# The second layer's modulation summed by VectorE and Pool instead of TensorE

## The chip, the core and the metric

The kernel runs on one core of a Trainium2 chip. The metric is the device time of one execution in microseconds. Engines are named as in the profile: PE is TensorE's matmul (PEld its weight load), DVE is VectorE, ACT is ScalarE, POOL is Pool, SP issues DMAs from its own queue.

## What is computed

One step of a trunk of two layers on 640 tokens (128 context tokens, 512 latents) with 1024 features. Each layer has a mixer and a convolutional FFN, and each of the two is wrapped in norms whose shift, scale and gate come from a conditioning vector. There are two conditions, one for the context and one for the latents. The part that the change touches is this one, for layer 1:

```
def modulation(cond, w_mod, b_mod):
    m = (jax.nn.silu(cond) @ w_mod + b_mod)[:, None, :]
    return jnp.split(m, N_MOD, axis=-1)
...
sh1p, sc1p, gt1p, sh2p, sc2p, gt2p = modulation(ctx_cond, w_mod, b_mod)
sh1s, sc1s, gt1s, sh2s, sc2s, gt2s = modulation(c, w_mod, b_mod)
```

w_mod is 1024 x 6144 in float32, 25 MB, read once; only two rows are multiplied with it. Six groups of 1024 columns give the six vectors.

## The kernel before

The activations lie feature-major, 128 features on the partitions, as pairs of a rounded high and a low part; a product takes three matmuls (low x high, high x high, high x low). `split` makes such a pair of a loaded weight: ScalarE rounds (L310), VectorE subtracts (L311). Weights come in units of 512 KB through a ring of three raw buffers, issued by SP (L320).

The FFN (`ffn`) goes over 22 pairs of 128 columns. `up` makes both halves of a pair: `conv` loads and splits a unit of w_up, `feat` (L678) multiplies it in 48 matmuls into a pair of PSUM banks, then ScalarE (L1212) and VectorE (L1213, L1214) evacuate the banks with the three taps of the convolution. There are two pairs of banks in turn, so the product after next needs the evacuation of this one. ScalarE and VectorE then join the two halves (L1222, L1223) and split the result. After three or four pairs `down` multiplies them with w_down (mm3, L327 to L329) in ten steps of 512 columns into two banks in turn, and VectorE adds each step to the sum (L1244).

Layer 1's modulation runs in the background of layer 0's FFN: `ffn` takes a step of the generator `bg` between the two products of a pair (three pairs take one more). A step of `mod_steps` loads two pieces of w_mod of 128 x 1024 (L383, a ring of two buffers "mraw") and multiplies them at once: the two conditions, padded to 32 columns, are the weights, and four matmuls with 512 columns stand side by side in four column groups of the array (L386). Eight steps sum a group of 2048 columns over the input features in PSUM, and three groups make the six vectors; at the end of a group ScalarE copies the bank (L391), four transposes turn it and VectorE adds bias and gains. The gates go to DRAM as rows by a Pool DMA (L457).

The instructions of each engine stand in the order that a scheduler gave them when the kernel was built; on the chip each engine and each DMA queue keeps that order and waits where data or a buffer is missing.

Of the kernel before, what the change touches and what calls it, by code (L numbers as in the profile page):

```python
# [19 lines left out]
ALU = mybir.AluOpType  # L20
# [65 lines left out]
def turns(*gens):  # L86
    """the generators' steps in turn."""
    gens = list(gens)
    while gens:
        for g in list(gens):  # L90
            try:
                next(g)
            except StopIteration:
                gens.remove(g)
                continue
            yield


def weave(main, side, n=1):
    """after each step of main, n steps of side; what is left of side at the end."""  # L100
# [6 lines left out]
def play(order, **gens):  # L107
    """a step of the generator that each letter names; what is left of them at the end."""
# [5 lines left out]
def skew(gens, every=1, n=0):  # L114
    """generator i starts every steps behind generator i - 1; the first has gone n steps."""
# [9 lines left out]
class Arena:  # L125
    """Places buffers in the stretches of SBUF it has been given: large ones as high as they fit, others in the room
    given back longest ago.  A new user of some room waits only for the earlier users of the same room."""
# [35 lines left out]
    def fit(self, cols, x):  # L163
        """the bottom of the smallest free room in stretch x that has cols."""
# [18 lines left out]
class Chunks:  # L183
    """chunks of 128 features on the partitions, kept as pieces."""
# [10 lines left out]
class Cols:  # L195
    """the same, as one piece per stretch of columns (piece j: columns starts[j] ..)."""
# [7 lines left out]
    def parts(self, c0, c1):  # L204
        """(a, b, piece, column in it): columns a .. b of c0 .. c1 as they lie in the pieces."""
# [6 lines left out]
class Kernel:  # L212
# [6 lines left out]
    def open(self, name, n, cols, dt=F32, order=None, top=False, at=None):  # L219
        """a ring of n slots (at: the stretch of each; as a tuple: at its end)."""  # L220
# [21 lines left out]
    def trim(self, name, keep):  # L242
        """gives back all slots but the keep last ones got."""
# [26 lines left out]
    def zone(self, name, side, arena, sizes, dt):  # L270
        """a stretch of SBUF for one arena; close_zone ends it."""
# [60 lines left out]
    def rstd(self, ss, n, scale):  # L332
        """(scale * ss + eps) ** -0.5 by three Newton steps."""
# [17 lines left out]
    def rstd1(self, ss, scale):  # L351
        """(scale * ss + eps) ** -0.5 of one column: ScalarE's root, VectorE's reciprocal and a Newton step."""
# [9 lines left out]
    def exp_ln(self, after):  # L362
        """ScalarE's table with both Exp and Ln, loaded behind an instruction of its."""
# [10 lines left out]
    def mod_steps(self, l, g):  # L374
        """2048 columns of silu(c) @ w_mod, four column groups side by side in the PE array; then what follows from them."""
# [32 lines left out]

    def mod_first(self, h, A, B, behind):
        """layer 0's first shift and scale for quarter h of the features."""  # L410
# [35 lines left out]
    def gate_rows(self, l, qb, cols, bcol, gcol):  # L446
        """(gate + b) * g_post of both conditions, written to DRAM as rows."""
# [11 lines left out]
    def gates(self, l, qb):  # L459
        """those rows, the same in all partitions: [P, 1024] per condition."""  # L460
# [6 lines left out]
    def transpose_mod(self, xt, xn, i, A, B, hi, lo, off, bank="un", act=False, dve=2):  # L467
        """rmsnorm, modulation and transposition of one token tile into hi / lo columns off.. (xn: scratch)."""
# [41 lines left out]
    def residual(self, xt, t, m, G, junk=None):  # L510
        """xt += G * rmsnorm(m)."""
# [39 lines left out]
    def operand(self, name, order=None):  # L551
        """a product's feature-major operand, as two parts (high, low) of two pieces each."""
# [4 lines left out]
    def operand_cols(self, name, starts, w):  # L557
        """the same, as one piece per stretch of w columns."""
# [4 lines left out]
    def start(self):  # L563
        """conditioning vectors, first modulation group, normalised and transposed inputs, layer 0's first operand."""
# [58 lines left out]
    def first_vectors(self, l, r):  # L623
        """the columns that the first modulation needs."""
# [5 lines left out]
    def other_vectors(self, l, r):  # L630
        """the other vectors of a layer: a step to load them as rows, one to turn them."""
# [565 lines left out]
    def ffn(self, l, h2, G, bg, pre, store, fin, post):  # L1197
# [57 lines left out]
        for gi, n in enumerate(gsz):  # L1255
            want = NF if gi == len(gsz) - 2 else min(NF, f0 + n + 1)
            while nx < want:
                up(nx)
                nx += 1
                if nx in (10, 14, 18):  # L1260
                    next(bg, None)
# [457 lines left out]
```

## Time and profile before

| | us |
|---|---|
| median of 3 runs | 1807.58 (1804.44 to 1813.03) |
| span of the profiled execution | 1802.6 |
| TensorE busy | 1759.0 (98%) |
| VectorE busy | 1033.5 (57%) |
| ScalarE busy | 727.8 (40%) |
| Pool busy | 73.8 (4%) |

The page gives the profiled execution's span, from its first to its last instruction; its median run is 5 us longer. Busy shares are means over stages with different limits; the stage that matters is layer 0's FFN, whose up and down products run from about 495 to 990 us.

### The profile page before, as it was taken

The page shows a single profiled execution, that of the slowest core. Times are in us where ns is not written, and L with a number is a line of the kernel's source. Part 1 is how long each engine was busy: PE and PEld are TensorE (multiplying, and loading weights), DVE is VectorE, ACT ScalarE, POOL GpSimd, SP SyncE. Part 2 cuts the span into 40 slices and gives each one's busy share as a digit, 9 for nine tenths or more (in the row PEclk, how much of TensorE's full clock was granted, in tenths as well). Part 3 has the DMA queues.
Part 4 walks back from the last instruction along what each step waited for, and adds up shares of the span by engine and source line. Part 5 has one row for each costly group of instructions (what it writes and reads, how often), then busy time and mean ns, then how long its engine had stood idle before and what let it go on. Part 6 is the DMA issues. An engine that isn't in the chain of part 4 may idle for free.

```text
span 1802.6 us, 26680 instructions
## 1 busy us (share of the span) xinstructions
PE 1759.0 (98%) x10810; PEld 1525.6 (85%) x10810; DVE 1033.5 (57%) x1950; ACT 727.8 (40%) x1291; POOL 73.8 (4%) x177
## 2 busy tenths in 40 slices
PE   6999999989999999999999999999999999999998
PEld 4787888757798989898988988887889989898996
DVE  5768763556753444444457875666574445454556
ACT  5554533324543323232335665556453313232332
POOL 2011131010000000000000000000000000000000
PEclk8999999868999999999999999999999999999999
DMA  9444331014433434343433110012352213132211
GB/s 309 132 128 137 108 115 52 24 43 134 149 127 108 140 95 163 94 164 94 164 126 117 55 42 26 10 36 89 122 187 71 82 47 105 47 100 67 81 59 59
DMA packets 161771, 180.67 MB, mean 100 GB/s; under 512 B 13493, under 2 KB 133696, under 8 KB 161648
## 3 DMA queue, kind: packets, MB, share of 16 engines
q1 hardware_dynamic: 157216, 169.11, 30.1%
q0 software_dynamic: 4432, 9.86, 1.5%
q8 instruction: 85, 1.39, 0.3%
q14 instruction: 38, 0.31, 0.1%
HBM read 167.69 MB, written 11.21 MB: 99 GB/s over the span
## 4 chain that ended last, share of the span: by engine, by line
PE 88%; DMA 4%; DVE 4%; ACT 2%; issue 1%; SPq 0%; POOL 0%; DVEq 0%; ACTq 0%; POOLq 0%
PE ps L678 38%; PE ps L327 12%; PE ps L328 11%; PE ps L329 11%; PE ps L386 3%; DMA zm<-in_l_w_mod 2%; PE ps L1530 2%; PE ps L1495 1%; PE ps L1524 1%; PE ps L1174 1%; PE ps L1171 1%; PE ps L487 1%; PE ps L933 1%; DMA out<-zn 1%; PE ps L1494 1%
## 5 line engine op out<-in xcount | busy, mean ns | idle before, releaser
L678 PE MATMUL ps<-zr 128*128 128x324 f32 (+1 forms) x3984 | 670.0, 313 | 2.4 <-ACT zr L310 1.4
L678 PEld LDWEIGHTS ps<-zr 128*128 128x128 f32 x3984 | 607.8, 188 | 30.4 <-issue 22.6
L310 ACT ACTIVATE zr<-zf 128x1024 fp32r<-128x1024 f32 (+5 forms) x207 | 196.9, 962 | 197.4 <-PE ps L328 161.6
L1213 DVE SCALAR_TENSOR_TENSOR zf<-ps,zf 128x644 f32<-128x644 f32 x88 | 78.2, 889 | 254.6 <-ACT zf L1212 254.6
L327 PE MATMUL ps<-zr,zn 128*128 128x512 f32 (+2 forms) x540 | 208.2, 386 | 1.4 <-DVE zr L311 0.8
L1212 ACT ACTIVATE zf<-ps,zf 128x644 f32<-128x644 f32 x88 | 78.3, 889 | 307.0 <-PE ps L678 307.0
L328 PE MATMUL ps<-zr 128*128 128x256 f32 (+2 forms) x578 | 178.9, 309 | 0.0
L328 PE MATMUL ps<-zr,zn 128*128 128x512 f32 x422 | 166.6, 395 | 0.0
L311 DVE TENSOR_TENSOR zr<-zf,zr 128x1024 fp32r<-128x1024 f32 (+4 forms) x126 | 135.9, 1082 | 46.8 <-ACT zr L310 43.3
L678 PE MATMUL ps<-zr,zn 128*128 128x324 f32 x672 | 159.5, 313 | 0.0
L327 PE MATMUL ps<-zr 128*128 128x256 f32 (+2 forms) x460 | 147.8, 321 | 1.8 <-ACT zf L1501 0.6
L1244 DVE TENSOR_TENSOR zm<-zm,ps 128x512 f32<-128x512 f32 x100 | 68.5, 686 | 112.7 <-PE ps L329 112.4
L329 PE MATMUL ps<-zr 128*128 128x256 f32 (+3 forms) x440 | 132.5, 301 | 0.0
L327 PEld LDWEIGHTS ps<-zr,zn 128*128 128x128 f32 x540 | 101.6, 188 | 24.5 <-DVE zm L1244 1.6
L678 PEld LDWEIGHTS ps<-zr,zn 128*128 128x128 f32 x672 | 113.9, 188 | 8.8 <-issue 5.9
L311 DVE TENSOR_TENSOR zn<-zf,zr 128x1024 fp32r<-128x1024 f32 (+3 forms) x81 | 92.9, 1151 | 43.1 <-ACT zr L310 40.6
L328 PEld LDWEIGHTS ps<-zr 128*128 128x128 f32 x578 | 110.6, 191 | 3.0 <-issue 0.4
L327 PEld LDWEIGHTS ps<-zr 128*128 128x128 f32 x460 | 87.9, 191 | 19.6 <-issue 9.6
L328 PEld LDWEIGHTS ps<-zr,zn 128*128 128x128 f32 x422 | 79.4, 188 | 18.1
L329 PE MATMUL ps<-zn,zr 128*128 128x320 f32 (+5 forms) x278 | 92.0, 333 | 0.0
L329 PE MATMUL ps<-zr,zn 128*128 128x512 f32 x222 | 87.8, 396 | 0.0
L329 PEld LDWEIGHTS ps<-zr 128*128 128x128 f32 x440 | 84.3, 192 | 1.3 <-DVE zr L311 0.3
(403 smaller groups left out, 2515.6 us busy)
## 6 DMA issues: line engine op xcount, KB each, us to landing
zf<-in_l_ffn_w_up SPq DMA_DIRECT2D x88, 512.0 KB, 3.9
zf<-in_l_w_mod SPq DMA_DIRECT2D x48, 512.0 KB, 4.7
zf<-in_l_ffn_w_down SPq DMA_DIRECT2D x44, 512.0 KB, 3.3
zm<-in_l_w_mod SPq DMA_DIRECT2D x32, 512.0 KB, 4.2
zf<-in_l_w_in SPq DMA_DIRECT2D x24, 512.0 KB, 4.7
zf<-in_l_w_out SPq DMA_DIRECT2D x16, 512.0 KB, 3.3
zm<-in_l_w_mod SPq DMA_DIRECT2D x26, 256.0 KB, 6.1
zf<-xd SPq DMA_DIRECT2D x10, 512.0 KB, 3.9
```

What stands on the lines that cost most here:

```text
L310: self.nc.scalar.activation(out=hi, in_=src, func=AF.Copy)
L311: self.nc.vector.tensor_tensor(out=lo, in0=src, in1=hi.bitcast(F32), op=ALU.subtract)
L327: mm(out=out, lhsT=al, rhs=bh, start=start, stop=False)
L328: mm(out=out, lhsT=ah, rhs=bh, start=False, stop=False)
L329: mm(out=out, lhsT=ah, rhs=bl, start=False, stop=stop)
L386: nc.tensor.matmul(out=ps[b:b + 32, :], lhsT=self.cT[:, k, :], rhs=r[:, 512 * q:512 * q + 512], start=k == 0, stop=k == KT - 1, tile_posit ...
L487: nc.tensor.transpose(out=ps[:, k, :], in_=xn[:, P * (k0 + k):P * (k0 + k) + P], identity=self.ident)
L678: self.nc.tensor.matmul(out=ps[:, j, :n], lhsT=w[:, k, :], rhs=hT[x][:, k, chunks[j]:chunks[j] + n], start=k == 0 and w is wl, stop=k == K ...
L1212: nc.scalar.activation(out=t, in_=ps[:, :, 1:HC + 1], func=AF.Identity, scale=cc[:, 1, ff:ff + 1], bias=cc[:, 3, ff:ff + 1])
L1213: nc.vector.scalar_tensor_tensor(out=t, in0=ps[:, :, 0:HC], scalar=cc[:, 0, ff:ff + 1], in1=t, op0=ALU.mult, op1=ALU.add)
L1244: nc.vector.tensor_tensor(out=acc[i][:, s], in0=acc[i][:, s], in1=ps, op=ALU.add)
L1530: nc.tensor.matmul(out=po, lhsT=v[1 + kt][x][:, hs], rhs=pt[y][:, tt], start=kt == 0 and x == 1, stop=kt == 5 and y == 1)
```

## The change

Layer 1's modulation no longer multiplies on TensorE piece by piece. `mod_steps_sum` goes over the six groups of 1024 columns. For each piece of 128 input features it loads 128 x 1024 of w_mod into a ring of three buffers and adds it, scaled by the condition's value of each partition, to a sum of 128 x 1024 per condition: VectorE does the first condition in one instruction, Pool the second in two, the first of them in place in the loaded buffer (so it waits for VectorE to have read it). When eight pieces are in, eight matmuls with a matrix of ones in one column add up the partitions, and the result is copied, turned and used as before. The background steps are now two, three and three pieces of a group, 19 in all, and the three additional steps of `ffn` are gone.

```diff
+    def mod_steps_sum(self, l):
+        nc = self.nc
+        w, v = self.a[f"l{l}_w_mod"], self.vcol[l]
+        sel = self.one("msel", [P, 2, 32])
+        nc.gpsimd.memset(sel, 0.0)
+        for c in range(2):
+            nc.gpsimd.memset(sel[:, c, c:c + 1], 1.0)
+        acc = [self.get("macc", [P, D]) for _ in range(2)]
+        def add(u, k):
+            r = self.get("mraw", [P, D])
+            nc.sync.dma_start(out=r, in_=w[P * k:P * k + P, D * u:D * u + D])
+            s = [self.cT[:, k, c:c + 1] for c in range(2)]
+            if k == 0:
+                nc.vector.tensor_scalar(out=acc[0], in0=r, scalar1=s[0], scalar2=None, op0=ALU.mult)
+                nc.gpsimd.tensor_scalar(out=acc[1], in0=r, scalar1=s[1], scalar2=None, op0=ALU.mult)
+            else:
+                nc.vector.scalar_tensor_tensor(out=acc[0], in0=r, scalar=s[0], in1=acc[0], op0=ALU.mult, op1=ALU.add)
+                nc.gpsimd.tensor_scalar(out=r, in0=r, scalar1=s[1], scalar2=None, op0=ALU.mult)
+                nc.gpsimd.tensor_tensor(out=acc[1], in0=r, in1=acc[1], op=ALU.add)
+        def finish(u):
+            ps = self.bank("um")
+            for c in range(2):
+                for q in range(4):
+                    nc.tensor.matmul(out=ps[32 * q:32 * q + 32, 0:256], lhsT=sel[:, c, :], rhs=acc[c][:, 256 * q:256 * q + 256],
+                                     start=c == 0, stop=c == 1, tile_position=(0, 32 * q))
+            R = self.get("R", [P, 256])
+            nc.scalar.copy(out=R, in_=ps[:, 0:256])
+            ps = self.bank("un")
+            for j in range(2):
+                nc.tensor.transpose(out=ps[:, P * j:P * j + P], in_=R[:, P * j:P * j + P], identity=self.ident)
+            m = self.get("mc", [P, 4, 2, 2])
+            nc.vector.tensor_copy(out=m, in_=ps[:, 0:256].rearrange("p (j q r) -> p q j r", j=2, q=4)[:, :, :, 0:2])
+            self.mod_piece(l, u, m.rearrange("p q j c -> p (q j) c"))
+        for u in range(6):
+            for a, b in ((0, 2), (2, 5), (5, 8)):
+                if a == 0 and u:
+                    finish(u - 1)
+                for k in range(a, b):
+                    add(u, k)
+                yield
+        finish(5)
+        yield
+    def mod_piece(self, l, u, m):
+        v = self.vcol[l]
+        b = v[:, 8 * u:8 * u + 8]
+        if u in (0, 3):
+            setattr(self, "B1" if u == 0 else "B2", self.shift(m, b))
+        elif u in (1, 4):
+            g = 48 if u == 1 else 56
+            setattr(self, "A1" if u == 1 else "A2", self.scale(m, b, v[:, g:g + 8]))
+        else:
+            g = 72 if u == 2 else 80
+            self.gate_rows(l, 0 if u == 2 else 2, m, b, v[:, g:g + 8])
...
             while nx < want:
                 up(nx)
                 nx += 1
-                if nx in (10, 14, 18):
-                    next(bg, None)
...
         self.set_banks(BANKS_MAIN)
-        self.open("mraw", 2, D)
+        self.open("macc", 2, D)
+        self.open("mraw", 3, D)
         G2 = self.gates(0, 2)
 
         def pre():
-            self.close("mraw", "R", "mc")
+            self.close("mraw", "macc", "msel", "R", "mc")
...
-        self.ffn(0, h2, G2, chain(*[self.mod_steps(1, g) for g in range(3)]), pre, store, fin, post)
+        self.ffn(0, h2, G2, self.mod_steps_sum(1), pre, store, fin, post)
```

Lines of the changed kernel are 62 higher behind this place: L1213, L1214, L1223, L521 and L477 of before are L1275, L1276, L1285, L583 and L539. Its adds are L426 and L429 on VectorE and L427, L430 and L431 on Pool, its loads L423, its finish L437, L443 and L445.

First place: VectorE behind the first down projection of layer 0's FFN. zf and zm hold float32 buffers, ps is PSUM, zr and zn hold operands. Before:

```order
L311 TENSOR_TENSOR zn_3573<-zf_58,zr_62 128x1024 x2
L311 TENSOR_TENSOR zr_62<-zf_58,zr_62 128x1024
L1213 SCALAR_TENSOR_TENSOR zf_58<-ps,zf_58 128x644
L311 TENSOR_TENSOR zr_62<-zf_58,zr_62 128x1024
L1214 SCALAR_TENSOR_TENSOR zf_58<-ps,zf_58 128x644
L1213 SCALAR_TENSOR_TENSOR zf_58<-ps,zf_58 128x644
L311 TENSOR_TENSOR zr_62<-zf_58,zr_62 128x1024
L1214 SCALAR_TENSOR_TENSOR zf_58<-ps,zf_58 128x644
```

With the change:

```order
L311 TENSOR_TENSOR zn_3573<-zf_58,zr_62 128x1024 x2
L311 TENSOR_TENSOR zr_62<-zf_58,zr_62 128x1024
L426 TENSOR_SCALAR zf_58<-zf_58 128x1024
L1275 SCALAR_TENSOR_TENSOR zm_87<-ps,zf_58,zm_87 128x644
L429 SCALAR_TENSOR_TENSOR zf_58<-zf_58 128x1024
L1276 SCALAR_TENSOR_TENSOR zm_87<-ps,zf_58,zm_87 128x644
L445 COPY zf_58<-ps 128x16
L429 SCALAR_TENSOR_TENSOR zf_58<-zf_58 128x1024
L498 TENSOR_TENSOR zf_58<-zf_58 128x16
L311 TENSOR_TENSOR zr_62<-zf_58,zr_62 128x1024
L429 SCALAR_TENSOR_TENSOR zf_58<-zf_58 128x1024 x2
L1275 SCALAR_TENSOR_TENSOR zm_87<-ps,zf_58,zm_87 128x644
```

Five of a group's eight adds stand between the start of one evacuation and the next but one; the other three follow before the second half of the third.

Second place: VectorE among the last token tiles of the output projection, before the FFN. Before:

```order
L311 TENSOR_TENSOR zr_62<-zf_58,zr_62 128x1024
L311 TENSOR_TENSOR zr_62<-zm_87,zr_62 128x4x63
L311 TENSOR_TENSOR zr_62<-zm_87,zr_62 128x4x67
L359 SCALAR_TENSOR_TENSOR zf_58<-zf_58 128x1
L521 SCALAR_TENSOR_TENSOR zm_87<-zm_87,zf_58 128x1024
L356 TENSOR_SCALAR zf_58<-zf_58 128x1
L357 RECIPROCAL zf_58<-zf_58 128x1
```

With the change:

```order
L359 SCALAR_TENSOR_TENSOR zf_58<-zf_58 128x1
L429 SCALAR_TENSOR_TENSOR zf_58<-zf_58 128x1024
L583 SCALAR_TENSOR_TENSOR zm_87<-zm_87,zf_58 128x1024
L429 SCALAR_TENSOR_TENSOR zf_58<-zf_58 128x1024
L356 TENSOR_SCALAR zf_58<-zf_58 128x1
L429 SCALAR_TENSOR_TENSOR zf_58<-zf_58 128x1024
L357 RECIPROCAL zf_58<-zf_58 128x1
L311 TENSOR_TENSOR zr_62<-zf_58,zr_62 128x1024
```

Three adds came in around the residual of a tile (L521, now L583) and the steps of its norm.

Third place: SP's queue of loads in the FFN. Before:

```order
L320 DMA zf_58<-in_l_ffn_w_up 128x8x128 x2
L383 DMA zf_58<-in_l_w_mod 128x1024 x2
L320 DMA zf_58<-in_l_ffn_w_up 128x8x128 x6
L383 DMA zf_58<-in_l_w_mod 128x1024 x2
L320 DMA zf_58<-in_l_ffn_w_down 128x1024 x2
L383 DMA zf_58<-in_l_w_mod 128x1024 x2
```

With the change:

```order
L320 DMA zf_58<-in_l_ffn_w_down 128x1024 x3
L320 DMA zf_58<-in_l_ffn_w_up 128x8x128 x8
L423 DMA zf_58<-in_l_w_mod 128x1024 x2
L320 DMA zf_58<-in_l_ffn_w_down 128x1024
L423 DMA zf_58<-in_l_w_mod 128x1024 x3
L320 DMA zf_58<-in_l_ffn_w_down 128x1024
L423 DMA zf_58<-in_l_w_mod 128x1024 x3
L320 DMA zf_58<-in_l_ffn_w_down 128x1024 x2
```

Loads of w_mod that wait for Pool stand in front of loads of w_down and w_up; they came in groups of two, waiting for TensorE, and now come in groups of two and three.

## Rows read from the trace of the kernel before

**Rows 1.** busy time by stage: from:to, length, busy us per engine (instructions).
```profile
core 0: us, PE busy (x) PEld busy (x) DVE busy (x) ACT busy (x) POOL busy (x), PEclk, DMA share, GB/s
440.00:495.00 55.00, 51.69 (x277) 43.44 (x277) 43.17 (x100) 29.05 (x56) 2.85 (x5) 1.00 0.49 162
495.00:930.00 435.00, 435.00 (x2671) 389.09 (x2672) 201.31 (x236) 134.56 (x159) 1.15 (x3) 1.00 0.40 128
```

**Rows 2.** who waited for whom from 466 to 930 us: total us, times, longest.
```profile
ACT zf L1212 <- PE ps L678: 159.2, 43, 6.5
DVE zf L1213 <- ACT zf L1212: 134.4, 41, 5.4
DVE zm L1244 <- PE ps L329: 41.5, 21, 2.1
```

**Rows 3.** the chain that ended last, 440 to 560 us: start, us, what.
```profile
471.45 1.30 DVE zm L521
472.77 1.16 ACT zm L472 x2
...
493.06 0.66 PE ps L487 x4
...
504.90 1.00 PE ps L386 x8
505.90 7.33 PE ps L678 x48
513.23 0.99 PE ps L386 x8
```

**Rows 4.** VectorE groups by form, 440-1000 us: busy us, mean ns, idle before.
```profile
L311 DVE TENSOR_TENSOR zr<-zf,zr 128x1024 fp32r<-128x1024 f32 x40 | 48.9, 1224 | 7.6 <-ACT zr L310 6.0
...
L1213 DVE SCALAR_TENSOR_TENSOR zf<-ps,zf 128x644 f32<-128x644 f32 x44 | 39.1, 889 | 138.8 <-ACT zf L1212 138.8
L1214 DVE SCALAR_TENSOR_TENSOR zf<-ps,zf 128x644 f32<-128x644 f32 x44 | 38.8, 882 | 0.0
...
L1223 DVE TENSOR_TENSOR zf<-zf 128x644 f32<-128x644 f32 x22 | 18.3, 830 | 14.6 <-ACT zf L1222 14.6
...
L521 DVE SCALAR_TENSOR_TENSOR zm<-zm,zf 128x1024 f32<-128x1024 f32 x5 | 6.4, 1284 | 0.1
...
L477 DVE TENSOR_SCALAR zm<-zm,zf 128x1024 f32<-128x1024 f32 x5 | 3.8, 754 | 0.2
```

**Rows 5.** Pool's groups by form, whole span.
```profile
L1009 POOL TENSOR_SCALAR_AFFINE_SELECT zf<-zf 128x256 bf16<-128x256 bf16 x2 | 1.9, 990 | 0.1
...
L606 POOL MEMSET zf<- 128x1024 f32 x1 | 0.9, 942 | 0.0
...
masks.py:199 POOL TENSOR_SCALAR_AFFINE_SELECT zf<-zf 128x128 f32<-128x128 f32 x1 | 0.3, 285 | 0.0
...
L539 POOL MEMSET zf<- 128x1 f32 x1 | 0.1, 99 | 0.0
```

**Rows 6.** the loads of w_mod (L383): issue in ns, landing in us.
```profile
L383 SPq DMA_DIRECT2D zf<-in_l_w_mod x48: 327/341/1281, 448.8 to 910.2; - x48
...
DMA to landing us min/median/max: 3.6/4.6/6.9
```

**Rows 7.** order of time: ScalarE near 537 us, VectorE near 642 us.
```profile
537.06 0.89 ACT L1212 ACTIVATE zf<-ps,zf 128x644 f32<-128x644 f32 x1 [2.05 <-PE ps L678]
...
641.96 0.69 DVE L1244 TENSOR_TENSOR zm<-zm,ps 128x512 f32<-128x512 f32 x1 [2.11 <-PE ps L329]
...
644.75 0.69 DVE L1244 TENSOR_TENSOR zm<-zm,ps 128x512 f32<-128x512 f32 x1 [2.10 <-PE ps L329]
```

**Rows 8.** order of time, 143 to 147 us: Pool, then VectorE.
```profile
144.03 1.94 POOL L1009 TENSOR_SCALAR_AFFINE_SELECT zf<-zf 128x256 bf16<-128x256 bf16 x2
...
144.66 1.05 DVE L955 TENSOR_TENSOR zn<-zn 128x640 f32<-128x640 f32 x1
```

**Rows 9.** instructions of L955: duration in ns min/median/max.
```profile
L955 DVE TENSOR_TENSOR zn<-zn x3: 815/826/1050, 139.6 to 220.2; 128x640 f32<-128x640 f32 x3
```


## Prediction

> **What bounds the kernel now.** I read the table by stage first. From 495 to 930 us, where the first FFN runs with the second layer's modulation in between, TensorE is busy 435.00 of 435.00 us at a granted clock of 1.00, VectorE 201 us, ScalarE 135 us, Pool 1.2 us [rows 1]. The waits of the same stretch say the same from the other side: ScalarE waits 159.2 us for L678's products, VectorE 134.4 us for ScalarE behind them and 41.5 us for the products of the down projection [rows 2]; nobody makes TensorE wait there. So what is taken off TensorE in this stretch is gained in full, as long as no other engine becomes late. Before 495 us it is different: in the chain of waits the pieces of 471 to 493 us are VectorE's, ScalarE's and TensorE's in turn [rows 3], with VectorE busy 43 of 55 us [rows 1].
>
> **What the change removes.** The chain of waits has one modulation step as a piece of its own between two up products: 1.00 and 0.99 us, with a product of 7.33 us behind the first [rows 3]. There are 24 such steps, eight for each of three groups, so 24 x 0.99 = 23.8 us of TensorE go.
>
> **What it adds on TensorE.** Six finishes of eight matmuls. One holds two rounds of four matmuls side by side with 256 columns; an old step holds one round of four with 512. That is the same number of columns in the same form, so I price a finish as a step: 6 x 1.0 = 6.0 us. Turning the results takes 6 x 2 transposes where it took 3 x 4, so nothing. Net on TensorE: 23.8 - 6.0 = 17.8 us, 1.0% of the span. If everything else were hidden, the time would be 1807.6 - 17.8 = 1789.8 us.
>
> **What it adds on VectorE.** Per group of 1024 columns one scaling and seven multiply-and-adds over 128x1024. Both forms are in the trace: L477 is 754 ns, L521 (two inputs and a scalar, all in SBUF) 1284 ns [rows 4]. 6 x (0.75 + 7 x 1.28) = 58 us. Spread over 435 us in which VectorE is busy 201 us that would hide. But it isn't spread: the order puts the eight adds of a group into the evacuations of three neighbouring up products (first order fence), 23 us of TensorE's time, in which VectorE has already 3 x (0.89 + 1.22 + 0.88) + 2 x 0.83 = 10.6 us of work [rows 4], and 9.7 us come. That fits with 2 us left, if no add waits.
>
> **What it adds on Pool, and the wait that comes with it.** Each add has a Pool part: a scaling of 128x1024, and from the second on an add of two 128x1024. The trace has no such instruction. The nearest rows: a memset of 128x1024 takes 942 ns, a float select over 128x128 285 ns, a bf16 select over 128x256 990 ns [rows 5]. With 0.1 us of fixed cost, the float select goes at 1.45 ns a column, the bf16 one at 3.5. That bounds the scaling by 0.94 and 3.7 us and the pair by 2.5 us (0.94 + 1.58) and 7.6 us; I take the float select's rate, 1.6 us, and half as much again for the second operand, 2.4 us: a pair of 4.0 us, an estimate. The loads of w_mod now wait for this: a buffer of three is free only when Pool has used it, and the load then takes 4.6 us to land [rows 6].
>
> I follow one group by hand, that of the first fence, from the end of up product a (time 0). The finish holds TensorE to 1.0. First add to 1.8, evacuation of a (first half) to 2.7, second add to 3.9, second half to 4.8, small copy, third add to 6.3, split of a weight to 7.7. The fourth add needs the first one's buffer: Pool 1.8 to 3.4, landed at 8.0, add to 9.3. The fifth needs the second one's: Pool 3.9 to 7.9, landed at 12.5, add to 13.8. Only then stands the evacuation of product b, which was ready at 9.2 (b ends at 8.3, ScalarE's part takes 0.89 us [rows 7]): with the split it ends at 16.8. Product d needs b's banks and is due when c ends, at 15.7: TensorE waits 1.1 us. Sixth add to 18.1; seventh: third buffer free at 11.9, fourth at 15.9, landed 20.5, add to 21.8; eighth: landed 24.5, to 25.8; second half of c's evacuation to 26.7, product e due at 24.1: 2.6 us more. Sum 3.7 us a group. The group at the end of the second up stage delays the first accumulation of the down projection instead (17.5 against 13.8, with 2.8 us a step, the distance of the two L1244 in [rows 7]): again 3.7 us. Five groups: 18.5 us. With Pool's pair at 2.5 us the same steps give 0 us for the first form and about 2 us for the second.
>
> The first group falls before 495 us, among the last tiles of the output projection, where VectorE is in the chain [rows 3]. It adds 9.7 us there, of which three stand among L521, L356 to L359 and L477 of one tile (second fence): I take half, 5 us, between 0 and 10. SP's queue has w_down and w_up loads behind the w_mod loads that wait for Pool (third fence), but the splits of these weights run four to five products ahead, some 30 us; I cost that at nothing as long as a group lasts under 35 us.
>
> **Pool and VectorE beside each other.** The trace has one place. Two selects of Pool run from 144.03 to 145.97; VectorE's L955 (two SBUF inputs, 128x640) starts at 144.66 and takes 1.05 us [rows 8], where the others of its line take 815 to 826 ns [rows 9]. So 0.22 us were lost by one VectorE instruction beside one Pool instruction of 1 us; the second select was not longer. In a group 13 VectorE instructions have two SBUF inputs (8 adds, 3 splits, L1223, the split after it), and Pool, with 30 us of work, is active nearly all the time. The lower price is 13 x 0.22 = 2.9 us a group; but Pool's new instructions are two to three times as long as that select and read two operands. If each of the 13 waited for half a Pool instruction of 2 us it would be 13 us. I take 0.45 us each, 5.9 us, nearer to the row, since these 13 stand in the chain that already sets the end of the group.
>
> **Sum for the forecast.** -17.8 + 5 x (3.7 + 5.9) + 8 (first group, 5 and 3 for the neighbourhood) = +38 us. The profiled span is 1802.6 us and the median of the runs 1807.58, 5.0 us above it; I carry the difference over: 1807.6 + 38 = 1846 us. With the lower price of the neighbourhood it is 1829.
>
> **Rivals.**
> *Pool-paced loads alone.* Nothing is lost side by side: -17.8 + 18.5 + 5 = +6, 1813 us; with a pair between 2.5 and 4.0 us, 1800 to 1813. For it: the second select of [rows 8] was not slowed. A page speaks for the cheaper half of it: the Trainium skill, "GPSIMD Engine Reference", section "Performance versus the Vector engine", has an fp32 add of 2048 in 4497 ns on this engine; half of that, an estimate, is 2.25 us for 1024, and with one-input work near line rate the pair would be about 3.3 us and this rival's time about 1805 us. No run here shows it yet.
> *All is hidden.* The pair takes 2.5 us or less and VectorE's adds fit: -17.8 + 2 + 3 = -13, 1795 us: faster. It decides whether the fifth add of a group is done before product b's banks are due. For it: TensorE's neighbours have 50% room on average [rows 1]; against it: the adds stand eight in 23 us, and three buffers with 4.6 us of landing allow one add per (4.6 + 1.3 + 2.5) / 3 = 2.8 us at best, 22 us for eight.
> *Whole turns.* VectorE's two-input instructions and Pool's exclude each other: a group then lasts 8 x (1.28 + 4.0) + 3 x 1.22 + 2 x 0.83 - 4.0 (the last Pool pair) = 43.6 us instead of 26.7, 17 us more, times five, with 18.5 + 8 - 17.8: about 1900 us; with a pair of 2.5 us, 33.1 against 22.9, about 1850. In the middle 1875 us. Against it: by whole turns L955 would have waited from 144.66 to 145.02, 0.36 us, and the second select would have ended later; the rows have 0.22 us and no delay [rows 8, 9]. The Trainium skill, "SBUF — State Buffer", section "Who interferes with whom", states just this rule: a VectorE instruction with two SBUF inputs contends with a GpSimd instruction that reads SBUF, the one that starts first keeps the shared pair for the whole instruction and the other blocks. By that rule the time would be this rival's; the trace agrees that there is a loss and not on its size.
>
> **Chances.** Forecast 0.35, Pool-paced loads alone 0.25, all hidden 0.20, whole turns 0.20. The range from 1797 to 1882 leaves out a bit more than half of the third and of the fourth at their outer ends. A measurement of this kernel can tell about 0.5% from no change (1798.5 to 1816.6). Slower: forecast and whole turns and a little of the second, 0.60; same: the rest of the second and some of the third, 0.23; faster: 0.17. As most cases lie on the slow side, the forecast's own range is 1829 to 1865.
>
> **What would show it.** In the profile after: the finish's 48 matmuls in place of the second layer's 96 of L386; TensorE no longer at 435 of 435 us but with gaps, in the stretch to 930 us, that end on VectorE's evacuation or accumulation; SP's w_mod loads released by Pool; VectorE's adds well over 1284 ns or with idle time before them that ends on a w_mod load. If L431 is about 1.5 us or less and the adds stay at 1284 ns, the forecast is wrong and the time under 1800. If adds and splits come to 2.5 us and more, it is the whole-turn case. It is also wrong if the first group, before 495 us, costs far from 5 us, since its price is the least founded.

## The result and the profile after

The changed kernel takes 1869.07 us (median of four runs, 1864.94 to 1882.54); the kernel before took 1809.19 us beside it. The ratio is 1.0356, with an interval of 1.0313 to 1.0399: 3.6% slower. The profiled execution has a span of 1868.8 us against 1802.6.

The page of the changed kernel: busy time of each engine, and four of its groups (busy us, mean ns of one, idle time before them and what ended it).

```profile
PE 1758.1 (94%) x10714; PEld 1542.6 (83%) x10714; DVE 1152.2 (62%) x2001; ACT 725.9 (39%) x1294; POOL 350.9 (19%) x270
...
L740 PE MATMUL ps<-zr 128*128 128x324 f32 (+1 forms) x3984 | 682.4, 317 | 39.8 <-DVE zm L1276 34.2
...
L430 POOL TENSOR_SCALAR zf<-zf 128x1024 f32<-128x1024 f32 x42 | 151.4, 3606 | 14.0 <-DVE zf L429 7.8
...
L429 DVE SCALAR_TENSOR_TENSOR zf<-zf 128x1024 f32<-128x1024 f32 x42 | 87.6, 2086 | 37.3 <-DMA zf<-in_l_w_mod 37.3
L431 POOL TENSOR_TENSOR zf<-zf 128x1024 f32<-128x1024 f32 x42 | 108.6, 2585 | 3.3
```

A Pool pair takes 3.61 + 2.59 = 6.2 us, not the 4.0 of the prediction. VectorE's add takes 2.09 us instead of the 1.28 of its form in [rows 4], and 37.3 us of idle time before the adds end on a w_mod load. TensorE now has idle time that ends on VectorE's second evacuation, L1276.

The table by stage, same stretches and columns as [rows 1]:

```profile
440.00:495.00 55.00, 44.39 (x222) 37.56 (x220) 49.53 (x85) 22.89 (x44) 36.09 (x16) 0.94 0.53 166
495.00:930.00 435.00, 379.95 (x2202) 349.96 (x2203) 268.05 (x245) 114.22 (x139) 223.60 (x74) 0.93 0.35 106
```

From 495 to 930 us TensorE is busy 379.95 of 435 us at a granted clock of 0.93, where before it was 435.00 at 1.00. What it waits for between 440 and 1010 us (us in total, times, longest), and what SP's loads of w_mod wait for:

```profile
PE ps L740 <- DVE zm L1276: 38.6, 6, 8.5
PE ps L327 <- DVE zm L1306: 11.1, 4, 5.4
PE ps L549 <- DVE zm L539: 7.5, 2, 6.6
PE ps L329 <- DVE zn L311: 5.9, 1, 5.9
```

```profile
SPq L423 <- POOL zf L431: 218.7, 39, 9.3
```

One of these waits, in time. First VectorE from 585.60 us, then Pool beside it, then TensorE (start, us, instruction; in brackets the idle time before it):

```profile
585.60 2.93 DVE L429 SCALAR_TENSOR_TENSOR zf<-zf 128x1024 f32<-128x1024 f32 x1 [0.42 <-DMA zf<-in_l_w_mod]
591.58 3.20 DVE L429 SCALAR_TENSOR_TENSOR zf<-zf 128x1024 f32<-128x1024 f32 x1 [3.06 <-DMA zf<-in_l_w_mod]
594.71 0.88 DVE L1275 SCALAR_TENSOR_TENSOR zm<-ps,zf,zm 128x644 f32<-128x644 f32 x1
595.50 1.33 DVE L311 TENSOR_TENSOR zr<-zf,zr 128x1024 fp32r<-128x1024 f32 x1
596.76 0.87 DVE L1276 SCALAR_TENSOR_TENSOR zm<-ps,zf,zm 128x644 f32<-128x644 f32 x1
597.60 3.43 DVE L429 SCALAR_TENSOR_TENSOR zf<-zf 128x1024 f32<-128x1024 f32 x1
```

```profile
587.42 3.82 POOL L430 TENSOR_SCALAR zf<-zf 128x1024 f32<-128x1024 f32 x1
591.32 2.37 POOL L431 TENSOR_TENSOR zf<-zf 128x1024 f32<-128x1024 f32 x1
593.67 3.82 POOL L430 TENSOR_SCALAR zf<-zf 128x1024 f32<-128x1024 f32 x1
597.57 2.37 POOL L431 TENSOR_TENSOR zf<-zf 128x1024 f32<-128x1024 f32 x1
```

```profile
592.57 0.75 PE L740 MATMUL ps<-zr 128*128 128x324 f32 x4
597.78 0.88 PE L740 MATMUL ps<-zr,zn 128*128 128x324 f32 x2 [4.46 <-DVE zm L1276]
598.46 1.28 PE L740 MATMUL ps<-zr 128*128 128x324 f32 x4
```

The add at 591.58 starts late because its piece lands late (3.06 us), and then lasts 3.20 us because Pool's add began 0.26 us earlier and holds it up to 593.5; its own 1.28 us come behind that. The evacuation L1275 and L1276, which is quick (0.88, 0.87 us), stands behind this add in VectorE's order, and TensorE stands idle for 4.46 us until it is done. Then TensorE runs at half speed: four matmuls take 1.28 us where they took 0.75. The granted clock of four stretches around the gap is the eighth column here:

```profile
590.00:592.90 2.90, 2.90 (x22) 2.90 (x21) 1.32 (x1) 0.00 (x0) 2.82 (x2) 1.00 0.59 242
593.50:597.70 4.20, 0.00 (x0) 0.00 (x0) 4.20 (x5) 0.03 (x1) 4.12 (x3) 1.00 0.43 125
597.80:600.90 3.10, 3.10 (x12) 3.10 (x13) 3.10 (x1) 0.61 (x1) 3.10 (x2) 0.50 0.00 0
601.20:605.00 3.80, 3.80 (x28) 3.80 (x27) 2.03 (x3) 2.47 (x3) 3.72 (x2) 1.00 0.33 127
```

To sum this over the FFN I take two stretches that every run has. **S1** goes from the first residual of layer 0's output projection (L520 of before) to the first matmul of L678 with the names ps<-zr,zn, among the first up products. **S2** goes from there to the first residual of layer 1's output projection. S2 of before, and of after (same columns):

```profile
505.80:1276.20 770.40, 766.52 (x4565) 667.60 (x4562) 422.74 (x730) 325.24 (x608) 9.40 (x22) 1.00 0.31 99
```

```profile
513.50:1342.50 829.00, 765.26 (x4475) 680.58 (x4474) 523.73 (x774) 325.60 (x611) 242.50 (x98) 0.97 0.28 86
```

S2 grew by 58.6 us and S1 from 68.4 to 82.9, by 14.5. The profiled run of after was 6.8 us earlier at the start of S1, before any add of the change, and behind S2 nothing differs (526.4 and 526.3 us): 58.6 + 14.5 - 6.8 = 66.3, the difference of the spans. In S2 TensorE has 90 matmuls less and is busy as long as before; its idle time went from 3.9 to 63.7 us.

### The profile page after: what moved, and what is told of

It reads as the page before. It is cut to its first block, busy times and chain, and to the rows that moved or that the text cites. A ratio compares the mean times of both kernels' runs of the same rounds, so it can differ in the third digit from the quotient of the medians.

```text
span 1868.8 us, 26697 instructions
## 1 busy us (share of the span) xinstructions
PE 1758.1 (94%) x10714; PEld 1542.6 (83%) x10714; DVE 1152.2 (62%) x2001; ACT 725.9 (39%) x1294; POOL 350.9 (19%) x270
## 4 chain that ended last, share of the span: by engine, by line
PE 67%; issue 13%; POOL 7%; DVE 6%; DMA 4%; ACT 2%; SPq 0%; DVEq 0%; POOLq 0%; ACTq 0%
PE ps L740 25%; PE ps L327 10%; PE ps L329 9%; PE ps L328 9%; POOL zf L430 4%; POOL zf L431 3%; PE ps L1590 2%; DMA zm<-in_l_w_mod 2%; PE ps L386 1%; PE ps L1555 1%; PE ps L549 1%; PE ps L1584 1%; PE ps L1233 1%; DMA zf<-in_l_w_mod 1%; PE ps L1236 1%
## 5 line engine op out<-in xcount | busy, mean ns | idle before, releaser
L740 PE MATMUL ps<-zr 128*128 128x324 f32 (+1 forms) x3984 | 682.4, 317 | 39.8 <-DVE zm L1276 34.2
L740 PEld LDWEIGHTS ps<-zr 128*128 128x128 f32 x3984 | 621.2, 192 | 57.2 <-issue 48.4
L328 PE MATMUL ps<-zr,zn 128*128 128x512 f32 x422 | 169.6, 402 | 0.0
L430 POOL TENSOR_SCALAR zf<-zf 128x1024 f32<-128x1024 f32 x42 | 151.4, 3606 | 14.0 <-DVE zf L429 7.8
L327 PEld LDWEIGHTS ps<-zr,zn 128*128 128x128 f32 x540 | 103.7, 192 | 39.9 <-DVE zm L1306 14.6
L311 DVE TENSOR_TENSOR zn<-zf,zr 128x1024 fp32r<-128x1024 f32 (+3 forms) x81 | 97.5, 1208 | 40.1 <-ACT zr L310 38.0
L740 PEld LDWEIGHTS ps<-zr,zn 128*128 128x128 f32 x672 | 115.1, 190 | 7.3 <-issue 6.3
L328 PEld LDWEIGHTS ps<-zr 128*128 128x128 f32 x578 | 110.2, 191 | 2.9 <-issue 0.2
L1275 DVE SCALAR_TENSOR_TENSOR zf<-ps,zf 128x644 f32<-128x644 f32 x44 | 39.1, 888 | 116.2 <-ACT zf L1274 116.2
L429 DVE SCALAR_TENSOR_TENSOR zf<-zf 128x1024 f32<-128x1024 f32 x42 | 87.6, 2086 | 37.3 <-DMA zf<-in_l_w_mod 37.3
L431 POOL TENSOR_TENSOR zf<-zf 128x1024 f32<-128x1024 f32 x42 | 108.6, 2585 | 3.3
L327 PEld LDWEIGHTS ps<-zr 128*128 128x128 f32 x460 | 87.7, 191 | 19.6 <-issue 9.4
L328 PEld LDWEIGHTS ps<-zr,zn 128*128 128x128 f32 x422 | 81.5, 193 | 18.4
L1274 ACT ACTIVATE zf<-ps,zf 128x644 f32<-128x644 f32 x44 | 39.2, 890 | 141.6 <-PE ps L740 141.6
```

Of the source, the lines that this page charges most:

```text
L311: self.nc.vector.tensor_tensor(out=lo, in0=src, in1=hi.bitcast(F32), op=ALU.subtract)
L327: mm(out=out, lhsT=al, rhs=bh, start=start, stop=False)
L328: mm(out=out, lhsT=ah, rhs=bh, start=False, stop=False)
L429: nc.vector.scalar_tensor_tensor(out=acc[0], in0=r, scalar=s[0], in1=acc[0], op0=ALU.mult, op1=ALU.add)
L430: nc.gpsimd.tensor_scalar(out=r, in0=r, scalar1=s[1], scalar2=None, op0=ALU.mult)
L431: nc.gpsimd.tensor_tensor(out=acc[1], in0=r, in1=acc[1], op=ALU.add)
```

## The experiments

The theories: **A, taking turns** (a VectorE instruction with two operands in SBUF and a Pool instruction that reads SBUF exclude each other; from the fifth run on A0 if for the whole of any Pool instruction, A1 if a Pool scaling does so for a part of its length only). **B, the pace** (the length of Pool's pair and the ring of three buffers set when loads, and the evacuations behind the adds, can go). **C, VectorE's burst** (eight adds in three products are too much even alone). All runs, with the stretches S1 and S2 of their profiled executions and TensorE's busy time and granted clock in S2. A ratio is against the kernel before as it ran beside that run (medians of 1804 to 1809 us). S1 and S2 come from one execution of each run, which starts S1 somewhere between 426 and 449 us, so the stretches compare more closely than the medians:

| run | median us | ratio to before | S1 | S2 | TensorE busy in S2 | clock |
|---|---|---|---|---|---|---|
| before | 1809.19 | | 68.4 | 770.4 | 766.5 | 1.00 |
| the change | 1869.07 | 1.036 (1.031 to 1.040) | 82.9 | 829.0 | 765.3 | 0.97 |
| e1_no_adds | 1782.13 | 0.987 (0.983 to 0.990) | 68.4 | 748.8 | 745.0 | 1.00 |
| e2_vec_only | 1789.14 | 0.991 (0.988 to 0.993) | 72.2 | 748.9 | 745.2 | 1.00 |
| e3_pool_only | 1821.88 | 1.009 (1.006 to 1.012) | 89.2 | 776.4 | 756.8 | 0.98 |
| e4_both_vec | 1793.01 | 0.993 (0.990 to 0.995) | 75.6 | 749.0 | 745.2 | 1.00 |
| e5_scale_only | 1799.97 | 0.997 (0.995 to 0.998) | 78.5 | 762.4 | 748.7 | 1.00 |
| e6_add_only | 1845.61 | 1.022 (1.019 to 1.025) | 82.4 | 803.1 | 756.7 | 0.97 |
| e7_memsets | 1808.09 | 1.003 (1.001 to 1.005) | 81.8 | 757.1 | 747.8 | 1.00 |
| e12_two_scalings | 1852.22 | 1.025 (1.021 to 1.029) | 80.3 | 814.1 | 760.7 | 0.97 |
| e10_immediate | 1859.69 | 1.030 (1.027 to 1.034) | 82.5 | 821.3 | 763.2 | 0.97 |
| e11_late_change | 1875.47 | 1.038 (1.035 to 1.041) | 66.4 | 847.4 | 769.7 | 0.95 |
| e9_late_vec | 1783.33 | 0.988 (0.987 to 0.990) | 68.7 | 750.3 | 745.1 | 1.00 |

**TensorE's gain by itself.** From piece 2 of a group on, nothing is added:

```diff
             else:
-                nc.vector.scalar_tensor_tensor(out=acc[0], in0=r, scalar=s[0], in1=acc[0], op0=ALU.mult, op1=ALU.add)
-                nc.gpsimd.tensor_scalar(out=r, in0=r, scalar1=s[1], scalar2=None, op0=ALU.mult)
-                nc.gpsimd.tensor_tensor(out=acc[1], in0=r, in1=acc[1], op=ALU.add)
+                pass
```

> Left out: the sums over input features from the second piece of a group on, on both engines (only the first piece is scaled, by VectorE for both conditions); all 48 loads and the six finishes stay. It measures what TensorE gains by itself. All theories alike: 1807.6 - 17.8 = 1790 us, with TensorE at 435 of 435 us from 495 to 930 and a granted clock of 1.00. If it were over 1800, the loads or the finishes would cost something that no theory has.

S2 is 748.8 us: the gain is 21.6 us, a little more than the 17.8 expected. The rest lies in the products: right behind a step a product takes 7.33 us [rows 3], behind other work 7.12 in the same trace, 0.21 us less:

```profile
655.89 7.12 PE ps L678 x48
```

A finish costs the product behind it about as much (nine matmuls take 1.53 us behind it, where 7.12 / 48 each would make 1.33). Against this run the changed kernel loses 80.2 us in S2 and 14.5 in S1.

**VectorE's part alone.** The two lines of `nc.gpsimd` in the diff above are taken out, VectorE's stays (and VectorE also scales the second condition's first piece).

> Left out: Pool's part from the second piece of a group on (the second condition's sum); VectorE's seven multiply-and-adds a group stay. Theory A (VectorE's instructions with two SBUF operands and Pool's take turns): nothing to take turns with, 1790 to 1795 us, adds at 1.28 us. Theory B (Pool's pair paces the loads): the same, 1790 to 1795. Theory C (eight adds within three products are too much for VectorE by themselves): over 1800, with TensorE waiting on VectorE's evacuations.

S2 is the same as without adds, S1 3.8 us longer. Theory C falls: VectorE's 42 adds cost nothing in the FFN.

**Pool's part alone.** The line of `nc.vector.scalar_tensor_tensor` is taken out.

> Left out: VectorE's adds from the second piece of a group on; Pool's pairs stay. Theory A: Pool's pair, about 5.2 us where VectorE doesn't hold it up, still takes turns with the splits, the joining of the halves and the hlo splits, five VectorE instructions a group in place of 13: about 5/13 of the time lost, 1790 + 30 = 1820 us, with splits still at up to 3 us. Theory B: nobody but Pool waits for the paced loads, so TensorE waits for nobody: 1790 to 1795 us, with splits at 1.22 us.

1821.88 us, close to the 1820 of taking turns, though not for that reason alone. No add of VectorE waits for the paced loads here, and still the splits grow. VectorE, and Pool beside it (L429 is Pool's scaling and L430 its add in this kernel):

```profile
604.17 2.81 DVE L311 TENSOR_TENSOR zn<-zf,zr 128x1024 fp32r<-128x1024 f32 x1
606.90 0.88 DVE L1275 SCALAR_TENSOR_TENSOR zm<-ps,zf,zm 128x644 f32<-128x644 f32 x1
608.58 0.83 DVE L1284 TENSOR_TENSOR zm<-zm 128x644 f32<-128x644 f32 x1 [0.81 <-ACT zm L1283]
```

```profile
603.50 2.40 POOL L430 TENSOR_TENSOR zf<-zf 128x1024 f32<-128x1024 f32 x1
605.87 3.82 POOL L429 TENSOR_SCALAR zf<-zf 128x1024 f32<-128x1024 f32 x1
```

The split at 604.17 waits for the end of Pool's add at 605.90, less some 0.15 us, and then takes its 1.22; the scaling behind the add, 2.84 us elsewhere, waits for the split in turn and is 3.82 us long. L1275, with one operand in PSUM, and L1284, which meets only the later part of the scaling, keep their length.

In S2, where these rows stand, the run is 27.6 us longer than without adds. In S1 it is 20.8 us longer, and there most of it is the pace after all, by way of SP's queue: a load of w_up stands behind three of w_mod that wait for Pool, ScalarE waits for it (SP's queue, then ScalarE), and TensorE then waits 13.1 us for L538 (L477 of before).

```profile
471.57 12.54 SPq L423 DMA_DIRECT2D zf<-in_l_w_mod  x3
```

```profile
491.21 1.06 ACT L310 ACTIVATE zr<-zf 128x1024 fp32r<-128x1024 f32 x1 [13.44 <-DMA zf<-in_l_ffn_w_up]
```

So the time agreed with theory A partly by luck. The change itself does not lose time this way: from 440 to 1010 us ScalarE waits 13.5 us in all for loads of w_up, against 12.7 in the kernel before.

**Both conditions on VectorE.** Pool does nothing; all is computed:

```diff
-                nc.gpsimd.tensor_scalar(out=r, in0=r, scalar1=s[1], scalar2=None, op0=ALU.mult)
-                nc.gpsimd.tensor_tensor(out=acc[1], in0=r, in1=acc[1], op=ALU.add)
+                nc.vector.scalar_tensor_tensor(out=acc[1], in0=r, scalar=s[1], in1=acc[1], op0=ALU.mult, op1=ALU.add)
```

> Nothing is left out: VectorE adds both conditions, Pool does nothing here. Two adds of 1.28 us a piece, 20.5 us a group, beside 10.6 us of other VectorE work within three products of 23 us: 8 us late, of which the two pairs of banks in turn hide up to one product of 7.3 us. Theories A and B: 1790 to 1808 us, 40 us and more faster than the change, although VectorE does twice the adds. Theory C: slower than the change, over 1870, since VectorE's burst is twice as long.

Twice the adds on VectorE, and S2 is 749.0 us: TensorE's whole gain stays. Only S1 is longer, by 7.2 us.

**Which instruction of Pool.** One run leaves out Pool's add, the other its scaling.

> Left out: Pool's add of each pair; Pool's scaling and all of VectorE's adds stay. In the trace of the changed kernel VectorE's two-input instructions that meet a scaling lose at most 0.9 us, those that meet a Pool add wait for its end. Theory A1 (a scaling keeps VectorE out only for its first 0.9 us of 2.85, an add for all of its 2.37): VectorE's adds at most 2.2 us, most at 1.28, time 1785 to 1800 us. Theory A0 (each Pool instruction keeps it out for its whole length): adds up to 4.1 us, 1820 us and more. Theory B (pace alone): a Pool part of 2.85 us paces hardly anything, 1790 to 1797, adds at 1.28.

> Left out: Pool's scaling of each pair (it adds the unscaled piece); Pool's adds and all of VectorE's adds stay. Theories A0 and A1: VectorE's and Pool's adds stand in turn, 8 x (1.28 + 2.37) = 29 us a group, with the splits and the joining 35 us, where three products last 23: 7 us or more a group after what the two pairs of banks hide, 1820 to 1835 us, adds and splits up to 3.6 us. Theory B: a Pool part of 2.4 us a piece paces nothing (my steps gave 0 to 2 us a group for 2.5 us), 1785 to 1797 us, adds at 1.28.

The scaling alone costs 13.5 us in S2 against VectorE's part alone, the add alone 54.2. VectorE's adds in the two runs (min/median/max ns), scaling alone and then Pool's add alone:

```profile
L429 DVE SCALAR_TENSOR_TENSOR zf<-zf x42: 1264/1345/2071, 448.0 to 870.0; 128x1024 f32<-128x1024 f32 x42
```

```profile
L429 DVE SCALAR_TENSOR_TENSOR zf<-zf x42: 1265/1343/3423, 448.2 to 913.0; 128x1024 f32<-128x1024 f32 x42
```

Beside a scaling of 2.84 us no add loses more than 2.07 - 1.28 = 0.8 us; beside Pool's add it loses up to 2.14. So A1 holds, and A0 falls for the scaling. Theory B falls as the only cause, by the group of the adds with Pool's add alone (mean ns of one, then idle time before them):

```profile
L429 DVE SCALAR_TENSOR_TENSOR zf<-zf 128x1024 f32<-128x1024 f32 x42 | 87.7, 2089 | 0.2
```

They wait 0.2 us in all, for no load, and are as long as in the change; 54 us are lost by turns alone. The time is above my 1820 to 1835; I had not counted the small two-input instructions behind the finish, which wait as well (a 128x16 of L497 takes 2.37 us), but haven't shown that they make the difference.

**Pool writes and reads nothing.** Three memsets of the buffer, three of the sum.

> Pool's pair is replaced by three memsets of the loaded buffer and three of the sum, 6 x 0.94 = 5.7 us, about the pair's length, which write SBUF and read nothing (so the second condition's sum is left out); loads wait for Pool as before. If only instructions of Pool that read take turns with VectorE's: adds at 1.28 us, and the time shows the pace alone. By the steps of the prediction with 5.7 us in place of 4.0, the fifth add of a group ends at 16.2 us and the eighth at 33, product b's banks come free 3.5 us late and the next ones 6.3: 10 us a group, 1835 to 1845 us. If writes take turns too: adds well over 1.28 us and the time near the change's 1869. If the pace is no cost at all: 1790.

VectorE's adds stay short (1269/1285/1348 ns), so a Pool instruction that only writes does not take turns with a two-input add. It did hold up a VectorE scaling of one large operand: L541 (L477 of before, 0.75 us) began within a row of memsets (its line first) and was done 0.54 us after the last of them (second line).

```profile
482.69 9.27 DVE L541 TENSOR_SCALAR zm<-zm,zf 128x1024 f32<-128x1024 f32 x1
```

```profile
490.45 0.97 POOL L433 MEMSET zf<- 128x1024 f32 x1
```

TensorE waited 8.1 us for it, the larger part of the 13.4 us that this run adds in S1. As a measure of the pace the run fails: the buffer comes free after its own three memsets, 2.8 us earlier than in the changed kernel, and VectorE's adds stand in other places of its order. So the pace was tried again, with both held.

**The pace with the order held.** Pool's add becomes a second scaling of the same piece:

```diff
                 nc.gpsimd.tensor_scalar(out=r, in0=r, scalar1=s[1], scalar2=None, op0=ALU.mult)
-                nc.gpsimd.tensor_tensor(out=acc[1], in0=r, in1=acc[1], op=ALU.add)
+                nc.gpsimd.tensor_scalar(out=acc[1], in0=r, scalar1=s[0], scalar2=None, op0=ALU.mult)
```

> Pool's add is replaced by a second scaling of the same loaded piece, written to the sum (so the second condition's sum is left out). VectorE's instructions stand in the same order as in the changed kernel, every buffer is held to the end of Pool's pair as there, and the pair is no shorter (2 x 2.85 = 5.7 us against 2.85 + 2.37 = 5.2); only the instruction of Pool that read two operands is gone. Theory B (the pair's length and the ring of three set the time; e7_memsets gave a buffer back 2.8 us earlier and let VectorE's order move): no change, 1860 to 1875 us. Theory A1 (Pool's add keeps VectorE out for its whole length, a scaling for 0.9 us): adds at most 2.2 us, 1805 to 1825 us.

1852.22 us: neither the 1860 to 1875 of theory B alone nor the 1805 to 1825 of A1 alone. VectorE's adds are short again, and what they lost in length they now wait for the load:

```profile
L429 DVE SCALAR_TENSOR_TENSOR zf<-zf 128x1024 f32<-128x1024 f32 x42 | 60.5, 1441 | 64.5 <-DMA zf<-in_l_w_mod 64.5
```

In the changed kernel the same group has 2086 ns a piece and 37.3 us of waiting. Against the run with the scaling alone, where Pool's part is half as long, S2 is 51.7 us longer, while VectorE is busy 478.4 us in it here and 478.5 there: a second scaling cost it nothing more in turns, and the 51.7 us are the pace. So both theories are right. The turns of Pool's add alone make 54 us in S2 and the pace alone 52, but the change, which has both and the scaling's turns (13.5), loses 80. I take it that they overlap because both delay the same adds and the same evacuations behind them; no run shows the overlap by itself. The runs with one Pool instruction also differ from the change in the order of fewer than 25 of VectorE's 2001 instructions.

**What makes the scaling long.** Pool scales by 0.5 instead of a value per partition.

> Pool scales by a constant 0.5 in place of the condition's value of each partition (so the second condition's sum is wrong); all else as in the changed kernel. It prices the scaling by itself. If the value of each partition makes it long: a scaling near the memset's 0.94 us, a pair of 3.3 us, and a time near e6_add_only's 1845.6, since Pool's adds still take turns with VectorE. If any float32 scaling of 128x1024 takes Pool 2.85 us: 1869, as the change.

The scaling takes 2.77 us at least, against 2.84: the value of each partition isn't the reason. The ratio's interval overlaps with that of the change.

**The first group's place.** The first group's first VectorE instruction is queued behind the third evacuation:

```diff
             if k == 0:
-                nc.vector.tensor_scalar(out=acc[0], in0=r, scalar1=s[0], scalar2=None, op0=ALU.mult)
+                with self.tc.issue_after(self.evac.ins) if u == 0 else nullcontext():
+                    nc.vector.tensor_scalar(out=acc[0], in0=r, scalar1=s[0], scalar2=None, op0=ALU.mult)
```

> Nothing is left out: the changed kernel, with VectorE's part of the first group behind the third evacuation of the up stage (as in e9_late_vec). In the changed kernel the first group costs 14.5 us between the first residual of the output projection and the first product with both kinds of operand, the other five (1346.9 - 1266.8) / 5 = 16 us each in the FFN. If a group costs by what it does to VectorE wherever it stands: 14.5 us go and 16 come, 1865 to 1875 us. If the place among the last tiles was the worse part of it: under 1860.

S1 falls to 66.4 us, S2 rises to 847.4: 16.5 us go and 18.4 come. The first group costs about as much in either place. The same edit on the kernel with both conditions on VectorE:

> Nothing is left out: both conditions on VectorE as in e4_both_vec, and the first group, which stood among the last tiles of the output projection, now starts behind the third evacuation of the up stage. From the first residual of layer 0's output projection (L520 of before) to the first product with both kinds of operand, e4_both_vec took 75.6 us, the run without adds 68.4; that difference should go: 1793 - 7 = 1786 us, 0.988 of before. If the group costs the same in its new place, 1793.

1783.33 us, 86 us under the change and 1.2% under the kernel before, and as fast as the run without adds. From 495 to 930 us, and VectorE's two adds there:

```profile
495.00:930.00 435.00, 433.77 (x2671) 405.08 (x2670) 311.39 (x343) 138.18 (x165) 2.72 (x5) 1.00 0.43 131
```

```profile
L430 DVE SCALAR_TENSOR_TENSOR zf<-zf 128x1024 f32<-128x1024 f32 x42 | 53.7, 1279 | 0.0
L431 DVE SCALAR_TENSOR_TENSOR zf<-zf 128x1024 f32<-128x1024 f32 x42 | 53.7, 1278 | 0.0
```

VectorE is busy 311 of 435 us, 110 more than before the change [rows 1]; every add takes 1.28 us and none waits for a load.

## Why the prediction was right, and where it was not

The sign, the engine and the place were right: TensorE has gaps that end on VectorE's evacuation and on the first accumulations, and SP's loads wait for Pool. 1869 us lies in the range, but above the forecast's own 1829 to 1865; the sum was +38 us where S1 and S2 together show +73. So the range held, and the sum under it was half the size. Term by term:

- **TensorE's gain**: 17.8 expected, 21.6 measured (S2, e1_no_adds). A step and a finish cost 1.0 us as priced. The sum left out what an interruption costs the product behind it, 0.21 us; with 24 steps gone and six finishes added that is 18 x 0.21 = 3.8, the difference.
- **VectorE's 58 us of adds hide**: right. S2 is 0.1 us longer with them, and 0.2 with twice as many.
- **Pool's pair of 4.0 us**: the term that was mis-sized. It is 2.84 + 2.37 = 5.2 us undisturbed and 6.2 in the change. The add was guessed well (2.4); the scaling, taken at the float select's rate (1.6), takes 2.84. It was inside the bounds of 0.94 and 3.7. The Trainium skill, "GPSIMD Engine Reference", section "Performance versus the Vector engine", has the figure for 2048 of which I took half, an estimate of 2.25 us for the add; the trace is near it (2.34 to 2.40 where nothing holds the add up). The near line rate that I put beside it for the scaling is not what the trace shows.
- **The pace, 3.7 us a group**: the pair in the steps was wrong. With 5.7 us they give 3.5 + 6.3, about 10 us a group; e12_two_scalings against e5_scale_only shows 51.7 / 5 = 10.3. That this fits so well is partly luck: 12.0 of the 51.7 us (760.7 - 748.7) are longer busy time of the same matmuls at the lower clock, which the steps don't have; the gaps alone are 7.9 us a group.
- **The neighbourhood, 5.9 us a group**: (762.4 - 748.9) / 5 = 2.7 for the scaling's turns and (829.0 - 814.1) / 5 = 3.0 for Pool's add in place of a second scaling, 5.7 together. That fits, but partly by luck: with no pace to hide behind, Pool's add alone costs 54.2 / 5 = 10.8 a group.
- **The first group, 5 + 3 us**: 14.5 measured, far from the 5 us that I had named as its least founded price. Pool's pair is in this too: VectorE's part alone costs 3.8.
- **What the sum lacked**: TensorE's clock. In S2 the same 4475 matmuls take 765.3 us in the change and 745.0 without adds, so 20.3 of the 80.2 us are matmuls that run at the lower clock behind a gap, and 59.9 are the gaps themselves.

With the measured sizes: -21.6 + 5 x (10.3 + 5.7) + 14.5 = +73 us, and 6.8 less for the earlier start of this run: +66, the difference of the spans. This has to come out, since the terms are differences of the same stretches, each taken in one order; taken in the other order the pace behind Pool's add is 829.0 - 803.1 = 25.9 us, not 51.7.

**Whole turns**, the rival at 1875 us, was nearest in time, and its mechanism is there for Pool's add. With a pair of 2.5 us I put it at 1850; e6_add_only is just that case, 1845.61. I had argued against it from L955, which lost 0.22 us where whole turns would have cost 0.36 [rows 8]. Later traces show that a waiting VectorE instruction goes on 0.14 to 0.19 us before Pool's record ends (591.58 + 3.20 - 1.28 = 593.50, with Pool's add ending at 593.69; 605.76 and 605.90 for the split of e3_pool_only). With that, 0.36 becomes 0.17 to 0.22: the loss of 0.22 that I read as evidence against the rule fits it. The selects don't: the first began 0.11 us after L960 (two SBUF operands, 0.84 us) and the second while L955 ran, and they took 994 and 985 ns; why neither was held up stays open. Of the signs I had set for this case, the adds' mean of 2.09 us is short of 2.5, but single adds go to 4.99 us and splits of weights to 2.63. The Trainium skill, "SBUF — State Buffer", section "Who interferes with whom", has the rule; the trace agrees for Pool's add (whole instruction), for the memsets beside two-input adds (a write does not contend) and for evacuations, which have one of their two large operands in PSUM (0.88 us beside Pool, as before). It does not agree for Pool's scaling, which keeps VectorE out for 0.8 to 0.9 us of 2.84.

**Pool-paced loads alone**, 1813 us, was half of the matter and far too cheap, again by the pair. **All is hidden**, 1795, needed a pair of 2.5 us; e6_add_only has one, and takes 1846, since this rival left the turns out.

## What to carry to other kernels

Work for Pool is not free of VectorE: before giving Pool an instruction that reads SBUF, count VectorE's instructions with two SBUF operands in the same stretch, and price each as if it waited for the end of a Pool add. Look at VectorE's scalings of one large SBUF operand too. Here VectorE alone with twice the work was 76 to 86 us faster than VectorE and Pool together. And bound an unseen instruction by its own kind: a ring's pace depends on the whole time for which its buffer is held, so an error of 1.7 us in the pair (5.7 in e12_two_scalings against 4.0) grew to 6.6 us a group.

## What the runs showed of the hardware that I had not expected

- A Pool scaling of 128x1024 in float32 takes 2.84 us, longer than its add of two such operands (2.34 to 2.40 us), and 2.77 us with a constant. But it holds up a VectorE add by at most 0.8 us and a split by 0.9 (e5_scale_only, 2.10 us against 1.22): the turn lasts a third of it.
- Turns can add up: the longest add of the change takes 4.99 us (748.16). Pool issues a DMA beside its start (748.00 to 748.57), then comes Pool's add (748.59 to 750.99), and the last 1.28 us of VectorE's add begin 0.9 us into the scaling behind that.
- An instruction of 128x16 waits as long as a large one: L504 takes 2.37 us behind Pool's add, and at most 0.18 us as L442 of the kernel before.
- A VectorE instruction with one large operand can take turns too, if that lies in SBUF: L539, a scaling of 128x1024, has 1430 ns in the mean in the change and 754 ns in [rows 4], and a row of memsets stretched one to 9.27 us in e7_memsets; evacuations from PSUM keep their length (0.87 to 0.89 us).
- A gap of 4.46 us on TensorE was followed by 3.1 us at a granted clock of 0.50 (1.2 GHz), then 1.00 again (2.4 GHz). Over S2 the longer matmuls cost a third of what the gaps cost (20.3 and 59.9 us).
